# A recurrence's output products in one batch, its scores as 64x64 tiles, and two low-rank gates as split products

## The chip, the cores and the metric

The kernel runs on one core of a Trainium2 chip. The metric is the device time of one execution in microseconds; less is better. The time before is a median of three runs.

## What is computed

One layer of an encoder: sequence 2048, width 1024, float32. The change touches the left one of two parallel head groups, RWKV-7 with 8 heads of 64:

```python
proj = rms_norm(h, norm_mix_w) @ w_in                    # (2048, 1024) @ (1024, 3328)
r, k, v, wd, ad, gd = split(p + (p_prev - p) * mu)       # 512, 512, 512, 64, 64, 128 columns
w_log = -softplus(-(w0 + tanh(wd) @ w_decay_up)) - 0.5   # low-rank gate 1: 64 -> 512
a     = sigmoid(a0 + ad @ a_up)                          # low-rank gate 2: 64 -> 512
g     = sigmoid(gd) @ g_up
S_t   = S_{t-1} (diag(w_t) - kk_t^T (a_t kk_t)) + v_t^T k_t ;   y_t = S_t r_t     # per head
y     = group_norm(y) * lnx_w + lnx_b + bonus ;   out = y * g
```

The other parts (differential attention, attention to memory tokens, an MLP of width 4096 and the norms) are as large or larger and stay as they are.

## The kernel before

The tokens are handled in four blocks of 512. `phase1` (lines 740 to 950) multiplies the normed tokens by `w_in`, one column tile of 128 at a time. Each float32 product there is split in three: weights and tokens are each kept as a high and a low part of type fp32r, and `inproj_stream` (L631, L632, L634) issues high x high, high x low and low x high, each 128x128 by 128x512. This stream of matmuls is the bulk of the stage; a generator hands it out one step at a time, and `run` puts pieces of the recurrence between its steps, at fractions of a stage that the pieces yield.

The recurrence works on units: a block has two units, each of two pairs (p = 0, 1) of heads, and a pair holds two heads on 64 partitions each (`hs`). So there are 8 units and 16 pairs. A unit goes through `prep` (features, scores, transposes, the inverse of a triangular matrix, merge) and, a stage later, `finish` (the scan and the output), while the next unit is in `prep`.

- `rwkv_features` (L286) computes the two gates: `psw` (L291) and `psa` (L300) are one float32 product each per pair, 64 rows deep, with `lwa` holding `w_decay_up` on partitions 0 to 63 and `a_up` on 64 to 127, and `wad` the gates' inputs likewise. The tile `wad` comes from `lead0` at the head of each block. The features `BK` are written for a head in two steps, `BK[hs, :, h]` (L323) and then `BK[hs, :, 1 - h]` (L324).
- `rwkv_scores` (L349) makes, for 4 chunks of 64 tokens at a time and each head, one product `BK` x `AR` of 64 rows, 128 output rows and 128 columns (L359), and masks it on VectorE into `A` (L362). The quarter of `A` that lies in the other head's rows and the first 64 columns is not used from here: `rwkv_merge` (L502) writes columns 0 to 63 of all rows again.
- `rwkv_scan` (L505) runs over the 8 chunks of a unit. For each chunk and pair: `se` is the state times a decay (L521, ScalarE, one instruction a head); `psu` is `A` x `UV` (L524); `psy` gets its first term, `AR` x state (L526); `psu` is copied into `UV` (L528); then `pss` is `BKt` x `UV` (L534), `psy` gets its second term, `A` x `UV` (L536), and the new state is written to `UV` of the next chunk (L542, VectorE, one instruction a head). Chunk c+1 needs the state of chunk c. `psy` is needed by `rwkv_out` alone, after the scan.
- `prep_x` (L231) transposes and norms the next block's tokens (L247, L254); while it runs, the stream of that block has no input.

A float32 product is two MATMUL records in the trace ("passes" below), an fp32r product is one. The order of instructions on each engine is set at build time by a planner that works with priorities (`urgent`, `high_priority`) and its own estimate of times; on the chip every engine then runs its list in order. Tiles with the same `tag` share buffers, and a later tile waits until an earlier one is no longer read.

## Time and profile before

| | |
|---|---|
| time before, median of 3 runs | 3757.99 us (3751.84 to 3759.37) |
| the profiled execution: its own time | 3768.81 us |
| the profiled execution: span from first to last instruction | 3767.1 us |
| TensorE (PE) matmul busy | 3581.6 us, 95% |
| VectorE (DVE) busy | 1957.9 us, 52% |
| ScalarE (ACT) busy | 1720.5 us, 46% |
| GpSimd (POOL) busy | 1464.5 us, 39% |
| mean granted TensorE clock | 0.968 of 2.4 GHz |

Phase 1 with the recurrence takes about the first 1250 us. "Busy" of TensorE is from records whose ends overlap, so the cost of a matmul is read from when the next one starts. In the timeline a row is one or more instructions of the same line in a row: start, duration of the whole group, line, operation, tiles, rows * columns of the array in use, size of the moving operand and count.

### The profile page before, as it was taken

What the parts mean: (1) busy time and instruction counts of PE and PEld (TensorE: products, weight loads), DVE (VectorE), ACT (ScalarE), POOL (GpSimd) and SP (SyncE); (2) the same over time, 40 slices, a digit from 0 to 9 for tenths busy, and PEclk for the clock granted to TensorE, in tenths of its full rate; (3) what the DMA queues carried; (4) which work ended last, traced back from release to release, by engine and by line L of the source; (5) the groups of instructions that cost most, each with busy time, mean ns of one, the idle gap of its engine ahead of it and who ended that gap; (6) DMA issues with size and microseconds to landing.
All of it is one profiled execution on the core that took longest, in us unless ns stands there. A gap on an engine that the chain in (4) does not pass through costs nothing. (4 is left out here: it accounts for less than half of the span.)

```text
span 3767.1 us, 57886 instructions
## 1 busy us (share of the span) xinstructions
PE 3581.6 (95%) x21297; PEld 2871.5 (76%) x21297; DVE 1957.9 (52%) x4093; ACT 1720.5 (46%) x3802; POOL 1464.5 (39%) x1195
## 2 busy tenths in 40 slices
PE   7999999999999878899999989999999999999998
PEld 5767766767777767678787777888878888888887
DVE  4456666666574636465566756666634332313132
ACT  5364464454455626554455765555543421212123
POOL 4424324423434534344435435343353332222225
PEclk9989999999999899999999999999999999999999
DMA  4343342333335674343324425232243331111113
GB/s 149 107 128 88 82 127 84 86 107 88 87 88 160 207 210 142 106 121 93 113 79 118 139 73 144 79 112 78 85 152 94 111 102 48 48 51 48 48 57 108
DMA packets 566066, 390.52 MB, mean 104 GB/s; under 512 B 65187, under 2 KB 491254, under 8 KB 565782
## 3 DMA queue, kind: packets, MB, share of 16 engines
q1 hardware_dynamic: 534134, 329.55, 30.5%
q10 hardware_dynamic: 28064, 50.35, 4.0%
q0 software_dynamic: 3584, 6.92, 0.8%
q8 instruction: 168, 2.75, 0.3%
q14 instruction: 116, 0.95, 0.1%
HBM read 311.14 MB, written 75.56 MB: 103 GB/s over the span
## 5 line engine op out<-in xcount | busy, mean ns | idle before, releaser
L170 POOL TENSOR_TENSOR wlo<-wraw,whi 128x512 fp32r<-128x512 f32 x520 | 689.5, 1327 | 1247.6 <-ACT whi L169 1218.6
L616 POOL TENSOR_TENSOR wlo<-wraw,whi 128x512 fp32r<-128x512 f32 x288 | 413.8, 1438 | 597.4 <-ACT whi L615 479.3
L169 ACT ACTIVATE whi<-wraw 128x512 fp32r<-128x512 f32 x520 | 327.9, 631 | 639.9 <-PE ps_dn L187 327.0
L186 PE MATMUL ps_dn<-hdh,whi 128*128 128x512 f32 x1024 | 402.1, 393 | 2.3 <-DVE t L1408 1.2
L187 PE MATMUL ps_dn<-hdl,whi 128*128 128x512 f32 x1024 | 401.8, 393 | 0.3 <-DVE hdl L1413 0.3
L188 PE MATMUL ps_dn<-hdh,wlo 128*128 128x512 f32 x1024 | 398.8, 393 | 3.3 <-POOL wlo L170 3.1
L186 PE MATMUL ps_up<-h2h,whi 128*128 128x512 f32 x1024 | 400.1, 391 | 1.0 <-DVE t L1408 0.9
L187 PE MATMUL ps_up<-h2l,whi 128*128 128x512 f32 x1024 | 400.7, 391 | 0.0
L188 PE MATMUL ps_up<-h2h,wlo 128*128 128x512 f32 x1024 | 395.3, 391 | 0.8 <-POOL wlo L170 0.8
L631 PE MATMUL ps_acc<-xhi,whi 128*128 128x512 f32 x832 | 343.7, 414 | 20.0 <-ACT carry L278 18.9
L634 PE MATMUL ps_acc<-xhi,wlo 128*128 128x512 f32 x832 | 343.8, 414 | 2.2 <-POOL wlo L616 2.0
L632 PE MATMUL ps_acc<-xlo,whi 128*128 128x512 f32 x832 | 340.3, 409 | 0.0
L615 ACT ACTIVATE whi<-wraw 128x512 fp32r<-128x512 f32 x288 | 181.2, 630 | 273.4 <-PE ps_acc L632 98.0
L1422 DVE TENSOR_TENSOR ht<-ht,ps_dn 128x512 f32<-128x512 f32 x128 | 87.8, 686 | 347.3 <-PE ps_dn L188 347.2
L1048 ACT ACTIVATE pt<-ps_s,nmx 128x512 f32<-128x512 f32 (+3 forms) x320 | 198.4, 621 | 142.4 <-DVE nmx L1047 117.9
L1047 DVE TENSOR_REDUCE nmx<-ps_s 128x1 f32<-128x512 f32 (+3 forms) x320 | 192.5, 606 | 75.6 <-PE ps_s L1044 71.6
L188 PEld LDWEIGHTS ps_dn<-hdh,wlo 128*128 128x128 f32 x1024 | 193.1, 189 | 45.3 <-POOL wlo L170 6.4
L186 PEld LDWEIGHTS ps_dn<-hdh,whi 128*128 128x128 f32 x1024 | 193.0, 188 | 41.8 <-issue 1.6
L186 PEld LDWEIGHTS ps_up<-h2h,whi 128*128 128x128 f32 x1024 | 192.1, 188 | 41.3 <-DVE t L1408 1.6
L187 PEld LDWEIGHTS ps_dn<-hdl,whi 128*128 128x128 f32 x1024 | 193.2, 189 | 39.8 <-DVE hdl L1413 0.5
L188 PEld LDWEIGHTS ps_up<-h2h,wlo 128*128 128x128 f32 x1024 | 192.4, 188 | 40.3 <-POOL wlo L170 1.5
L187 PEld LDWEIGHTS ps_up<-h2l,whi 128*128 128x128 f32 x1024 | 192.3, 188 | 38.8
(336 smaller groups left out, 7772.4 us busy)
## 6 DMA issues: line engine op xcount, KB each, us to landing
wraw<-in_w_in_dram SPq DMA_DIRECT2D x208, 256.0 KB
wraw<-in_w_down_dram SPq DMA_DIRECT2D x208, 256.0 KB
wraw<-in_w_up_dram SPq DMA_DIRECT2D x192, 256.0 KB
s_hT<-xt ACTq DMA_DIRECT2D x64, 256.0 KB
wraw<-in_w_out_dram SPq DMA_DIRECT2D x56, 256.0 KB
s_qkvT<-qkv ACTq DMA_DIRECT2D x48, 256.0 KB
wraw<-in_w_mq_dram SPq DMA_DIRECT2D x48, 256.0 KB
wraw<-s_mb SPq DMA_DIRECT2D x48, 256.0 KB
```

The source lines that it names most:

```text
L169: nc.scalar.activation(out=hi, in_=raw, func=AF.Copy)
L170: nc.gpsimd.tensor_tensor(out=lo, in0=raw, in1=f32(hi), op=ALU.subtract)
L186: nc.tensor.matmul(ps, whi(k), ahi(k), start=(k == 0), stop=False)
L187: nc.tensor.matmul(ps, whi(k), alo(k), start=False, stop=False)
L188: nc.tensor.matmul(ps, wlo(k), ahi(k), start=False, stop=(k == nk - 1))
L615: nc.scalar.activation(out=hi, in_=raw, func=AF.Copy)
L616: nc.gpsimd.tensor_tensor(out=lo, in0=raw, in1=f32(hi), op=ALU.subtract)
L631: nc.tensor.matmul(o, hi[:, kk, :], xs[k][0], start=(k == 0), stop=False)
L632: nc.tensor.matmul(o, hi[:, kk, :], xs[k][1], start=False, stop=False)
L634: nc.tensor.matmul(o, lo[:, kk, :], xs[k][0], start=False, stop=last)
L1047: nc.vector.tensor_reduce(out=nmx[:, m, c:c + 1], in_=ps[:, 0:w], axis=AX.X, op=ALU.max, negate=True)
L1048: nc.scalar.activation(out=pt[:, cw(c)], in_=ps[:, 0:w], func=AF.Exp, bias=nmx[:, m, c:c + 1], accum_out=sm[:, m, c:c + 1])
```

## The change

- **Scan.** The two `psy` products leave the loop over chunks. The state at the start of every chunk is kept in a new tile `Sv` (128 x 8 x 64), written by one more VectorE instruction per chunk and pair, and `se` is read from it with one instruction for both heads. After the last chunk, all 16 `AR` x `Sv` products of a pair and then all 16 `A` x `UV` products are issued into `psy`. The scan yields two more steps, and the start of `rwkv_out` in `finish` moves from 17 to 19 units of `fscan`.
- **Scores.** The product of 128 output rows becomes two of 64: rows of the same head with all 128 columns, and rows of the other head with the last 64 columns alone. The mask becomes two instructions as well.
- **Gates.** `lead0` splits the gates' inputs into `wads`, two tiles with the high part on one half of the partitions and the low part on the other. `lora_load` keeps each second-layer weight twice over on 128 rows, as a high and a low tile. A gate product is then two fp32r matmuls 128 rows deep.
- The descriptor memory of GpSimd's DMAs is set to 2048 bytes.

```diff
+def lora_mm(g, ps, i, cs, wad):
+    for j in range(2):
+        g.nc.tensor.matmul(ps, g.lora[i][j][:, cs], wad[i], start=(j == 0), stop=(j == 1))
 def rwkv_features(...):
-    nc.tensor.matmul(psw, g.lwa[0:64, cs], wad[0:64, :], start=True, stop=True)
+    lora_mm(g, psw, 0, cs, wad)
-    nc.tensor.matmul(psa, g.lwa[64:128, cs], wad[64:128, :], start=True, stop=True)
+    lora_mm(g, psa, 1, cs, wad)
 def rwkv_scores(...):
-                nc.tensor.matmul(pss[h][:, cc, :], u.BK[hs, c, :, :]..., u.AR[hs, c, :, :]..., start=True, stop=True)
+                vs = slice(64 - 64 * h, 128 - 64 * h)
+                nc.tensor.matmul(pss[h][hs, cc, :], u.BK[hs, c, h, :], u.AR[hs, c, :, :]..., start=True, stop=True)
+                nc.tensor.matmul(pss[h][vs, cc, 64:128], u.BK[hs, c, 1 - h, :], u.AR[hs, c, 1, :], start=True, stop=True)
-            nc.vector.tensor_tensor(out=u.A[:, 4 * c4:4 * c4 + 4, h, :], in0=pss[h], in1=g.mask..., op=ALU.mult)
+            nc.vector.tensor_tensor(out=u.A[hs, cs, h, :], in0=pss[h][hs], in1=g.mask[hs...], op=ALU.mult)
+            nc.vector.tensor_tensor(out=u.A[vs, cs, h, 64:128], in0=pss[h][vs, :, 64:128], in1=g.mask[vs...], op=ALU.mult)
 def rwkv_scan(...):
+        u.Sv = sp.tile([P, NCK, CH], F32, tag=f"Sv{p}", name="Sv", bufs=1)
+        nc.scalar.activation(out=u.Sv[:, 0, :], in_=g.S[hp], func=AF.Copy)
-            for hs in H:
-                nc.scalar.activation(out=u.se[hs, :], in_=u.UV[hs, c, hs], func=AF.Copy, scale=u.EC[hs, c:c + 1])
+            nc.scalar.activation(out=u.se, in_=u.Sv[:, c, :], func=AF.Copy, scale=u.EC[:, c:c + 1])
-                nc.tensor.matmul(u.psy[hs, c, :], u.AR[hs, c, 1, :], u.UV[hs, c, hs], start=True, stop=False)
-                nc.tensor.matmul(u.psy[hs, c, :], u.A[:, c, h, 64:128], u.UV[:, c, hs], start=False, stop=True)
+                nc.vector.scalar_tensor_tensor(out=u.Sv[:, c + 1, :], in0=pss, scalar=u.EC[:, c:c + 1], in1=u.se, ...)
+    for p in range(2):
+        u.psy = g.ps_y.tile([P, NCK, CH], F32, tag=f"y{p}", name=f"psy{p}")
+        for c in range(NCK):
+            for hs in H:
+                nc.tensor.matmul(u.psy[hs, c, :], u.AR[hs, c, 1, :], u.Sv[hs, c, :], start=(c == 0), stop=False, ...)
+        for c in range(NCK):
+            for h, hs in enumerate(H):
+                nc.tensor.matmul(u.psy[hs, c, :], u.A[:, c, h, 64:128], u.UV[:, c, hs], start=False, stop=True, ...)
+        yield
 def lead0(blk):
-                t = pool.tile([P, TB], F32, tag="wad", name="wad", bufs=1)
+                t = pool.tile([P, TB], F32, tag="mix", name="wad", bufs=2)
+                for i, (r, o) in enumerate(((slice(0, 64), slice(64, 128)), (slice(64, 128), slice(0, 64)))):
+                    w = pool.tile([P, TB], F32R, tag=("wad", "wad1")[i], name="wads", bufs=1)
+                    nc.scalar.activation(out=w[r, :], in_=t[r, :], func=AF.Copy)
+                    nc.vector.tensor_tensor(out=w[o, :], in0=t[r, :], in1=f32(w[r, :]), op=ALU.subtract)
 def lora_load():
-            g.lwa = g.cst.tile([P, TB], F32, name="lwa")
-            nc.sync.dma_start(out=g.lwa[0:64, :], in_=g.i.w_decay_up[0])
-            nc.sync.dma_start(out=g.lwa[64:128, :], in_=g.i.a_up[0])
+            for nm, src in (("w", g.i.w_decay_up), ("a", g.i.a_up)):
+                raw = pool.tile([P, TB], F32, tag="mix", name="lraw", bufs=2)
+                for r in (0, 64):
+                    nc.sync.dma_start(out=raw[r:r + 64, :], in_=src[0])
+                nc.scalar.activation(out=hi, in_=raw, func=AF.Copy)
+                nc.gpsimd.tensor_tensor(out=lo, in0=raw, in1=f32(hi), op=ALU.subtract)
 def finish(u, sc=1.0):
-            t = 0.01 + g.fscan * 17
+            t = 0.01 + g.fscan * 19
-    nc = _bacc.Bacc("TRN2", target_bir_lowering=False, num_devices=1)
+    nc = _bacc.Bacc("TRN2", target_bir_lowering=False, num_devices=1, dynamic_dma_scratch_size=2048)
```

## Rows read from the trace of the kernel before

**Rows 1.** Busy time by stretch: PE, PEld, DVE, ACT, POOL, granted clock, DMA share, GB/s.
```profile
0.00:1200.00 1200.00, 1131.91 (x9333) 838.50 (x9333) 712.87 (x1794) 588.78 (x1411) 457.17 (x426) 0.95 0.37 105
```
**Rows 2.** Waits of PE, 100 to 1200 us: total, times, longest.
```profile
PE ps_acc L631 <- ACT carry L278: 13.8, 9, 2.1
```
**Rows 3.** Timeline of PE around two turns of the scan (start, duration, line, tiles, count).
```profile
391.95 0.39 PE L631 MATMUL ps_acc<-xhi,whi 128*128 128x512 f32 x1
392.18 0.40 PE L632 MATMUL ps_acc<-xlo,whi 128*128 128x512 f32 x1
392.50 0.34 PE L524 MATMUL psu<-UV,A 128*64 128x64 f32 x4
392.77 0.33 PE L526 MATMUL psy<-UV,AR 64*64 64x64 f32 x4
393.03 0.50 PE L634 MATMUL ps_acc<-xhi,wlo 128*128 128x512 f32 x1
...
393.69 0.32 PE L526 MATMUL psy<-UV,AR 64*64 64x64 f32 x2
393.95 0.34 PE L524 MATMUL psu<-UV,A 128*64 128x64 f32 x4
```
**Rows 4.** PE by line, 0 to 1300 us: count of passes, busy us, mean ns, idle before.
```profile
L359 PE MATMUL ps_sc<-AR,BK 64*128 64x128 f32 x512 | 74.0, 309 | 4.3 <-DVE A L362 3.9 <-ACT ta L302 0.4
L526 PE MATMUL psy<-UV,AR 64*64 64x64 f32 x512 | 67.0, 248 | 0.2
L536 PE MATMUL psy<-UV,A 128*64 128x64 f32 x512 | 54.4, 239 | 3.2 <-ACT UV L528 3.2
```
**Rows 5.** Timeline of PE, a turn of the scan with pss and the second psy term.
```profile
508.79 0.34 PE L534 MATMUL pss<-UV,BKt 128*64 128x64 f32 x4
508.95 0.29 PE L536 MATMUL psy<-UV,A 128*64 128x64 f32 x4
509.17 0.50 PE L634 MATMUL ps_acc<-xhi,wlo 128*128 128x512 f32 x1
```
**Rows 6.** DVE and ACT by line, 0 to 1300 us (columns of rows 4).
```profile
L362 DVE TENSOR_TENSOR A<-ps_sc,mask 128x512 f32<-128x512 f32 x64 | 43.0, 689 | 64.7 <-PE ps_sc L359 64.2
L538 DVE SCALAR_TENSOR_TENSOR S<-pss,EC,se 128x64 f32<-128x64 f32 x16 | 4.4, 277 | 8.5 <-PE pss L534 4.3 <-PE psy L536 4.1
...
L521 ACT ACTIVATE se<-UV,EC 64x64 f32<-64x64 f32 x256 | 88.5, 346 | 45.4 <-DVE UV L542 40.6 <-ACT se L521 0.2
```
**Rows 7.** Timeline of PE, one gate product and the next stream matmul.
```profile
354.13 1.12 PE L291 MATMUL psw<-wad,lwa 64*128 64x512 f32 x2
355.18 0.50 PE L632 MATMUL ps_acc<-xlo,whi 128*128 128x512 f32 x1
```
**Rows 8.** Timeline of PE, the stream's first wait after the start.
```profile
43.36 0.77 PE L631 MATMUL ps_acc<-xhi,whi 128*128 128x512 f32 x1 [5.13 <-ACT carry L278]
```
**Rows 9.** Timeline of PE, scores of both heads in one run, then of one.
```profile
400.18 1.16 PE L359 MATMUL ps_sc<-AR,BK 64*128 64x128 f32 x16
401.27 0.51 PE L634 MATMUL ps_acc<-xhi,wlo 128*128 128x512 f32 x1
...
511.50 1.16 PE L359 MATMUL ps_sc<-AR,BK 64*128 64x128 f32 x8
512.59 0.34 PE L524 MATMUL psu<-UV,A 128*64 128x64 f32 x4
```
**Rows 10.** Timeline of PE, 64x64 products on all four quarters of the array.
```profile
199.29 1.16 PE L500 MATMUL psw<-T,BK 64*64 64x64 f32 x64
```
**Rows 11.** Busy time by stretch, sum of the four stretches without stream (columns of rows 1).
```profile
sum 135.30, PE 121.64 PEld 87.15 DVE 107.02 ACT 93.81 POOL 19.98; mean PE 30.41 PEld 21.79 DVE 26.75 ACT 23.45 POOL 4.99
```
**Rows 12.** Timeline of PE, the stream after 3.7 us of small products.
```profile
385.40 0.63 PE L631 MATMUL ps_acc<-xhi,whi 128*128 128x512 f32 x1
385.82 0.63 PE L632 MATMUL ps_acc<-xlo,whi 128*128 128x512 f32 x1
```
**Rows 13.** DMAs that GpSimd issues: count, size, median us to landing.
```profile
LD<-A POOLq DMA_DIRECT2D x16, 128.0 KB, 2.9
```

More of the change, by code (lines that the diff above doesn't have):

```diff
@@ L358, in rwkv_scores @@
                 hs = slice(64 * h, 64 * h + 64)
-                nc.tensor.matmul(pss[h][:, cc, :], u.BK[hs, c, :, :].rearrange("p a t -> p (a t)"),
+                vs = slice(64 - 64 * h, 128 - 64 * h)
+                nc.tensor.matmul(pss[h][hs, cc, :], u.BK[hs, c, h, :],
                                  u.AR[hs, c, :, :].rearrange("p a t -> p (a t)"), start=True, stop=True)
+                nc.tensor.matmul(pss[h][vs, cc, 64:128], u.BK[hs, c, 1 - h, :], u.AR[hs, c, 1, :], start=True, stop=True)
+        cs = slice(4 * c4, 4 * c4 + 4)
         for h in range(2):
-            nc.vector.tensor_tensor(out=u.A[:, 4 * c4:4 * c4 + 4, h, :], in0=pss[h],
-                                    in1=g.mask[:, None, :].to_broadcast([P, 4, P]), op=ALU.mult)
+            hs, vs = slice(64 * h, 64 * h + 64), slice(64 - 64 * h, 128 - 64 * h)
+            nc.vector.tensor_tensor(out=u.A[hs, cs, h, :], in0=pss[h][hs],
+                                    in1=g.mask[hs, None, :].to_broadcast([64, 4, P]), op=ALU.mult)
+            nc.vector.tensor_tensor(out=u.A[vs, cs, h, 64:128], in0=pss[h][vs, :, 64:128],
+                                    in1=g.mask[vs, None, 64:128].to_broadcast([64, 4, 64]), op=ALU.mult)
         yield
@@ L510, in rwkv_scan @@
         u, hp = us[p], pairs[p]
+        u.Sv = sp.tile([P, NCK, CH], F32, tag=f"Sv{p}", name="Sv", bufs=1)
         for hs in H:
             nc.scalar.activation(out=u.UV[hs, 0, hs], in_=g.S[hp][hs, :], func=AF.Copy)
+        nc.scalar.activation(out=u.Sv[:, 0, :], in_=g.S[hp], func=AF.Copy)
     yield
-    for p in range(2):
-        us[p].psy = g.ps_y.tile([P, NCK, CH], F32, tag=f"y{p}", name=f"psy{p}")
     for c in range(NCK):
@@ L524, in rwkv_scan @@
                 nc.tensor.matmul(psu[hs, :], u.A[:, c, h, 0:64], u.UV[:, c, hs], start=True, stop=True)
-            for h, hs in enumerate(H):
-                nc.tensor.matmul(u.psy[hs, c, :], u.AR[hs, c, 1, :], u.UV[hs, c, hs], start=True, stop=False)
             for h, hs in enumerate(H):
@@ L534, in rwkv_scan @@
                 nc.tensor.matmul(pss[hs, :], u.BKt[:, c, hs], u.UV[:, c, hs], start=True, stop=True)
-            for h, hs in enumerate(H):
-                nc.tensor.matmul(u.psy[hs, c, :], u.A[:, c, h, 64:128], u.UV[:, c, hs], start=False, stop=True)
             if c == NCK - 1:
@@ L543, in rwkv_scan @@
                                                    in1=u.se[hs, :], op0=ALU.mult, op1=ALU.add)
+                nc.vector.scalar_tensor_tensor(out=u.Sv[:, c + 1, :], in0=pss, scalar=u.EC[:, c:c + 1],
+                                               in1=u.se, op0=ALU.mult, op1=ALU.add)
+        yield
+    for p in range(2):
+        u = us[p]
+        u.psy = g.ps_y.tile([P, NCK, CH], F32, tag=f"y{p}", name=f"psy{p}")
+        for c in range(NCK):
+            for hs in H:
+                nc.tensor.matmul(u.psy[hs, c, :], u.AR[hs, c, 1, :], u.Sv[hs, c, :], start=(c == 0), stop=False,
+                                 skip_group_check=True)
+        for c in range(NCK):
+            for h, hs in enumerate(H):
+                nc.tensor.matmul(u.psy[hs, c, :], u.A[:, c, h, 64:128], u.UV[:, c, hs], start=False, stop=True,
+                                 skip_group_check=True)
         yield
@@ L783, in post @@
             def post(ps):
-                t = pool.tile([P, TB], F32, tag="wad", name="wad", bufs=1)
+                t = pool.tile([P, TB], F32, tag="mix", name="wad", bufs=2)
                 mix_tile(g, pool, 12, ps, t, blk)
                 nc.scalar.activation(out=t[0:64, :], in_=t[0:64, :], func=AF.Tanh)
-                st[blk][1] = t
+                pair = []
+                for i, (r, o) in enumerate(((slice(0, 64), slice(64, 128)), (slice(64, 128), slice(0, 64)))):
+                    w = pool.tile([P, TB], F32R, tag=("wad", "wad1")[i], name="wads", bufs=1)
+                    nc.scalar.activation(out=w[r, :], in_=t[r, :], func=AF.Copy)
+                    nc.vector.tensor_tensor(out=w[o, :], in0=t[r, :], in1=f32(w[r, :]), op=ALU.subtract)
+                    pair.append(w)
+                st[blk][1] = pair
             return Item(blk, w_in(12), post, pre)
```

4 lines of the change are left out of this document (added).

## The prediction

> **What bounds the kernel now.** I read the stages first, then the waits of TensorE, then its timeline. In the first 1200 us, where the recurrence runs, TensorE is busy for 1131.9 us, VectorE for 712.9, ScalarE for 588.8 and GpSimd for 457.2 [rows 1]. The longest kind of wait of TensorE between 100 and 1200 us is 13.8 us in all [rows 2]. So a microsecond taken off TensorE's list there should come off the end, and the other engines have room, on average. Busy time hides what a small product costs, since records overlap; I take the time from one start to the next. The stream's matmuls start 0.23 us apart (391.95, 392.18) [rows 3]. A turn of the scan that stands between them costs more than its four passes: from the stream matmul at 392.18 to the one at 393.03 there are 0.85 us, where 0.23 would do, and the next one is some 0.1 us longer than usual [rows 3]. Every change of the array's shape has a price: a pass of these lasts about 0.24 us by itself [rows 4], so in a group of four that lasts 0.34 the last one started 0.10 us after the first, and the next shape began 0.15 us or more after that (392.50 to 392.77) [rows 3]. In a long run the step is smaller: 64 passes on four quarters of the array last 1.16 us [rows 10], (1.16 - 0.24) / 15 = 0.06 us for each on a quarter.
>
> **The y products leave the loop.** The first term has 512 passes [rows 4], four to a turn, so 128 turns. Where the four stand together they cost 0.26 us (392.77 to 393.03); where the two heads fall on either side of `psu` each half costs 0.26 us (393.69 to 393.95) [rows 3]. Walking the order of matmuls I count 203 groups of L526, so 203 x 0.26 = 53 us go. The second term, also 512 passes [rows 4], has the shape of `pss`, next to which it stands: a pair of passes costs 0.06 us, four 0.12 (from 508.95 to 509.17 are 0.22 us with the step back to the stream, which `pss` alone would pay too) [rows 5]; 128 x 0.12 = 15, and 16 with some groups that stand apart. The number of visits to the scan does not fall: `psu` and `pss` stay. What is added is a batch for each of the 16 pairs: 16 couples of passes at 0.06 for each term is 1.9 us, two shape changes 0.3 and the second-pass delays 0.1, so 2.3 us, 37 in all (34 if both pairs of a unit share a visit, 45 if the stream cuts in). Net: -53 - 16 + 37 = -32 us. The batch stands before `rwkv_out` of the unit alone, whose start the change moves later; nothing on TensorE waits for that but the tail of the last unit, so I add nothing.
>
> The first-term couples write one PSUM bank from two row halves. The trace has that already: four passes on both halves take 0.33 us as a group, two on one half 0.32 [rows 3], so they run side by side. The Trainium skill, TensorEngine Tiling (Array Packing), section Restrictions and Gotchas, says that row tiles cannot access one bank at the same time; by that rule each couple would take twice 0.06 us. The trace does not agree with it here.
>
> **VectorE and ScalarE in the scan.** 112 writes of `Sv` are added, at 0.28 us as the 128x64 update (L538), 31 us; 128 of the 256 `se` instructions go, at 0.35 us, 44 us off ScalarE; 16 copies come [rows 6]. VectorE's next instruction behind an `Sv` write is the other pair's state, and its `psu` waits 0.28 us more; the stream covers that while there is one.
>
> **The gates.** One product takes 1.05 us now (354.13 to 355.18) [rows 7]; each of 16 pairs has one for either gate: 32 x 1.05 = 33.6 us. Two stream-like matmuls at 0.23 [rows 3] are 0.46, in all 14.7, and they need no change of shape beside the stream: -19, of which 1 goes back since scan turns that now share a visit with a gate get one of their own: -18 us (-23 to -14). The splits in `lead0` are two instructions on ScalarE and two on VectorE for each of four blocks, ahead of products that come a stage later; the stream covers them. At the start, two more DMAs stand on SP's queue ahead of the first weights, and the first two normed tiles of `prep_x`, which share the tag `mix`, wait until GpSimd has made the low parts. Behind that comes a wait of 5.13 us of TensorE for ScalarE [rows 8], which can take up the delay: 0 to +5, I take +2.
>
> **Scores.** A head's eight passes of 128 columns cost 1.09 us as a run, and sixteen passes of both heads cost the same 1.09 (511.50 to 512.59, 400.18 to 401.27) [rows 9]: what counts is the length of one quarter's list. The new list of a quarter is eight passes of 128 columns, so it gets no shorter; the second product has its own quarter and can run beside it, as all four quarters do in L500 [rows 10]. The shape is cheaper to enter and leave by some 0.1 us a run; 69 runs are -7 us. But the second product needs the features of L324, the first those of L323 alone. If it is issued after the first it costs its eight passes at 0.06 and possibly a visit of 0.4 us, 0.87 together, for 64 heads of 4 chunks: up to +56. Near the gate of the features I expect a fifth of them to stand alone, +11 - 7, so +4. The 64 masks become 128 instructions; the added ones are bounded by the 128x64 and the 128x512 rows, 0.28 and 0.69 us [rows 6], I take 0.45: 29 us on VectorE.
>
> **Where there is no cover.** Four stretches of 26 to 40 us, where `prep_x` runs and the stream has no input, hold 28% of the scan's passes. There VectorE is busy for 107 of 135 us, TensorE for 122 [rows 11]. Of the 69 us taken off, 19 lie there; VectorE gets 28% of 31 + 29, so 17 us, and would stand at 124 of 135. I let half of TensorE's gain be lost there: +9 (0 to +28).
>
> **The clock.** After 3.7 us of small products the stream's matmuls are 0.43 us apart instead of 0.23 [rows 12]: the granted clock is at 1.2 GHz, half of 2.4, for some 3.4 us, and 1.6 us are lost. The batch of a unit is 4.5 us of small products. If each of eight brought that on: +13; the scan's shorter turns could save as much as 5. I take +4.
>
> **GpSimd's DMAs.** The smaller descriptor memory shows in no row. If each of its DMAs had to wait for the one before, that is some 2.9 us a piece [rows 13] in the chain of the inverse, which the stream covers; none to +10, I take 0, as TensorE waits little for that chain.
>
> **The sum.** -32 (y) - 18 (gates) + 2 (start) + 4 (scores) + 9 (no cover) + 4 (clock) = -31 us against the profiled execution's 3768.8. That one is 0.3% over the median of 3758, so the prediction is 3758 - 31 = **3727 us**.
>
> **Rivals.** (1) *Everything converts*: the heads' scores run side by side, the clock holds, the uncovered stretches shrink with TensorE. Then -32 - 18 - 7 = -57, 3701 us. For it: TensorE's 122 of 135 us; against it VectorE's load there. (2) *The uncovered stretches turn into VectorE's*: they lose all of the 19 us and grow by the 17 that VectorE gets, with the clock's +13: -32 - 18 + 2 + 4 + 36 + 13 = +5, 3763 us, no change. (3) *Slower: the second score product stands by itself.* The place is L359's successor in `rwkv_scores`, the price 0.87 us for each of 64. It takes up the gain without scores, 35 us, from 40 of 64 on, and the kernel is measurably slower from 49 of 64; with all, 3758 - 35 + 56 = 3779 us. For it: L324 is an instruction of 512 elements like the mask, some 0.69 us [rows 6], long enough for the first product's run to begin before it ends; against it: for the second group of four chunks all features are there. (4) *The batch does not run in couples*, two row halves taking turns at one bank: 16 pairs x 16 couples x 0.06 = +15 us, 3742 us; the groups of four and of two speak against it [rows 3]. This is the case that the Trainium skill's sentence above would make.
>
> **Chances.** The forecast with its own range of 3712 to 3748, in which (4) lies too, 0.58, of which (4) has 0.04; (1) 0.12; (2) 0.17; (3) 0.13. A difference under 0.2%, 7.5 us, can't be told from no change by this measurement. So faster 0.70, within 0.17, slower 0.13. The range that leaves 2 in 10 out runs from (1)'s end to just past (2): 3698 to 3767.
>
> **What would show it.** Right: scan visits of `psu` alone at four passes; the y products in 16 runs of some 2.3 us; gate products as two matmuls 0.23 apart; VectorE's idle time gone in the four stretches, which keep their length within 5 us. Wrong: score passes of the second kind in runs of their own; half clock right behind each batch; a stage after phase 1 that is longer than before, which would mean that the planner's new order, not the products, decides.

## The result, and the profile after

The changed kernel takes 3785.0 us (3780.2 to 3787.7, four runs) against 3758.7 us (3751.8 to 3764.8) of the kernel before beside it: a ratio of 1.0062, 95% interval 1.0033 to 1.0090, so some 23 us slower. The forecast was 3727 us with a range to 3767. The profiled execution has a span of 3782.5 us and a mean granted clock of 0.957 (before 3767.1 and 0.968). The profiled execution of the kernel before took 3768.81 us, 10 us more than its median, so between the two profiles there are only 15 us.

The first 1200 us by engine, columns as in [rows 1]:

```profile
0.00:1200.00 1200.00, 1089.64 (x9537) 822.06 (x9539) 760.33 (x1944) 538.37 (x1282) 448.25 (x420) 0.91 0.36 102
```

TensorE is busy for 42 us less than in [rows 1] and ScalarE for 50 less; VectorE has 47 us more. The granted clock has fallen from 0.95 to 0.91. So TensorE's list did get shorter, and the time went into gaps and into periods at a lower clock.

PE by line, 0 to 1300 us (columns of [rows 4]):

```profile
L365 PE MATMUL ps_sc<-AR,BK 64*64 64x128 f32 x512 | 78.0, 327 | 6.1 <-ACT ss L345 2.5 <-ACT ta L307 2.0 <-DVE BK L328 0.9
L367 PE MATMUL ps_sc<-AR,BK 64*64 64x64 f32 x512 | 56.5, 269 | 0.0
L534 PE MATMUL psu<-UV,A 128*64 128x64 f32 x512 | 47.1, 266 | 17.4 <-DVE Sv L550 17.3
L558 PE MATMUL psy<-Sv,AR 64*64 64x64 f32 x512 | 47.0, 264 | 0.4 <-DVE y L576 0.4
L562 PE MATMUL psy<-UV,A 128*64 128x64 f32 x512 | 25.4, 232 | 0.0
```

`psu` now waits 17.3 us, in 18 waits that end with VectorE's write of `Sv`; in the kernel before it had no such wait. The writes and the masks in two parts, by line of VectorE, 0 to 1300 us:

```profile
L371 DVE TENSOR_TENSOR A<-ps_sc,mask 64x512 f32<-64x512 f32 x64 | 43.8, 685 | 38.5 <-PE ps_sc L367 38.1
L550 DVE SCALAR_TENSOR_TENSOR Sv<-pss,EC,se 128x64 f32<-128x64 f32 x112 | 31.8, 284 | 1.6
L373 DVE TENSOR_TENSOR A<-ps_sc,mask 64x256 f32<-64x256 f32 x64 | 27.0, 422 | 1.4
```

Two turns of the scan in the timeline of PE (columns of [rows 3]):

```profile
515.13 0.34 PE L534 MATMUL psu<-UV,A 128*64 128x64 f32 x4
515.40 0.33 PE L558 MATMUL psy<-Sv,AR 64*64 64x64 f32 x4
515.66 0.34 PE L534 MATMUL psu<-UV,A 128*64 128x64 f32 x4
515.92 0.33 PE L558 MATMUL psy<-Sv,AR 64*64 64x64 f32 x4
```

The first y term stands behind `psu` just as in [rows 3]. In the text of the kernel it comes after the loop, but its operands are ready in the loop, and the planner has put many of them back: of the 152 runs of L558 (L526 had 203) 92 are groups of four passes, and 79 of these stand right behind `psu`. Of the second term most is a batch, here with 28 of a pair's 32 passes:

```profile
272.35 0.33 PE L558 MATMUL psy<-Sv,AR 64*64 64x64 f32 x4
272.61 1.04 PE L562 MATMUL psy<-UV,A 128*64 128x64 f32 x28
```

The gates came as predicted: matmuls 0.23 us apart behind the first, in place of 1.05 us for each product [rows 7]:

```profile
362.64 0.50 PE L288 MATMUL psw<-wads,lwh 128*128 128x512 f32 x1
362.97 0.39 PE L288 MATMUL psw<-wads,lwl 128*128 128x512 f32 x1
363.20 0.39 PE L288 MATMUL psw<-wads,lwh 128*128 128x512 f32 x1
```

The four stretches without stream, columns of [rows 1]. First the rows of the kernel before, of which [rows 11] has the sum, then those of the changed kernel:

```profile
222.50:256.70 34.20, 31.44 (x213) 23.63 (x211) 29.23 (x53) 21.85 (x56) 3.81 (x3) 0.63 0.49 157
510.00:545.60 35.60, 32.59 (x275) 23.15 (x273) 29.89 (x57) 24.32 (x65) 5.40 (x7) 0.85 0.47 145
800.90:826.70 25.80, 21.97 (x231) 15.35 (x229) 17.58 (x37) 19.42 (x48) 4.43 (x6) 0.97 0.67 180
1071.00:1110.70 39.70, 35.65 (x330) 25.02 (x329) 30.31 (x81) 28.22 (x84) 6.34 (x9) 0.80 0.38 95
```

```profile
225.40:264.00 38.60, 31.22 (x252) 21.87 (x250) 36.91 (x81) 23.01 (x62) 2.65 (x3) 0.62 0.49 151
514.40:551.60 37.20, 27.41 (x229) 19.47 (x227) 34.47 (x73) 19.92 (x53) 2.74 (x3) 0.63 0.52 156
806.70:834.70 28.00, 21.66 (x184) 15.46 (x182) 27.54 (x60) 17.73 (x46) 1.62 (x1) 0.64 0.41 136
1081.50:1127.80 46.30, 37.91 (x338) 25.85 (x336) 42.51 (x107) 26.50 (x80) 5.11 (x7) 0.59 0.24 67
sum 150.10, PE 118.19 PEld 82.65 DVE 141.43 ACT 87.16 POOL 12.13; mean PE 29.55 PEld 20.66 DVE 35.36 ACT 21.79 POOL 3.03
```

They are 15 us longer, VectorE (third figure) is busy for 141 of 150 us, and the clock, which had fallen far only in the first of them, is at 0.59 to 0.64 in all four: TensorE runs at 1.2 GHz there for most of the time. TensorE is idle for 32 of the 150 us (14 of 135 before); by its waits, some 18 us of that are for VectorE and some 10 for ScalarE, the longest 4.6 us. Waits are not all there is to it: in the first stretch of the kernel before the clock was at 0.63 as well, with this one wait (total, times, longest):

```profile
PE ps_xt L247 <- DVE xn L254: 2.8, 1, 2.8
```

In the whole profile the time at 1.2 GHz rose from 241 to 325 us, and single periods of 17 us or more, of which there was one, are now four, one in each stretch. The later phases keep their length: from the last 128x512 product of the first stream to the end there are 2352 us before and 2348 after.

### The profile page after: what moved, and what is told of

It reads as the page before. It is cut to its first block, busy times and chain, and to the rows that moved or that the text cites. A ratio compares the mean times of both kernels' runs of the same rounds, so it can differ in the third digit from the quotient of the medians.

```text
span 3782.5 us, 58913 instructions
## 1 busy us (share of the span) xinstructions
PE 3562.5 (94%) x21809; PEld 2872.0 (76%) x21809; DVE 2011.5 (53%) x4277; ACT 1676.9 (44%) x3700; POOL 1465.9 (39%) x1197
```

## The experiments

Every kernel was compared with the kernel before on the same chip (whose median differs between chips, 3757 to 3768 us). In the table, **lost** is (1 - mean granted clock) x span, median over the executions, as a difference to the kernel before (for the changed kernel, to the profiled execution of before): what the time at 1.2 GHz takes from TensorE's cycles, whether it needed them or not. **Rest** is the difference of the medians less that. The last three columns come from the one profiled execution, up to the start of the last 128x512 product of the first stream: idle time of PE, half of the time at 1.2 GHz, and what is left, TensorE's work at full clock. Idle time that lies at 1.2 GHz is in both of the last two columns: 13 us in the kernel before, 33 in the changed one, so work comes out up to some 10 us too low where that is much. For kernels whose TensorE products are the same the work differs by some 10 us (before, e_deadsv, e_shift, e_nofwd: 1232 to 1243) to 20 (e_ybatch, e_svpool, e_seuv: 1203 to 1223), so differences under 10 us say nothing, and those under 20 little.

| kernel | ratio, 95% interval | lost | rest | work | idle | half |
|---|---|---|---|---|---|---|
| before | 1 | 0 | 0 | 1234 | 100 | 82 |
| changed | 1.0062 (1.0033 to 1.0090) | +38 | -12 | 1172 | 140 | 123 |
| e_ybatch | 1.0077 (1.0057 to 1.0097) | +27 | 0 | 1214 | 127 | 96 |
| e_yforce | 1.0085 (1.0064 to 1.0107) | +37 | -4 | 1208 | 128 | 106 |
| e_lora | 0.9993 (0.9979 to 1.0008) | +19 | -21 | 1216 | 102 | 97 |
| e_scores | 1.0002 (0.9985 to 1.0020) | -4 | +3 | 1237 | 109 | 61 |
| e_noar | 1.0026 (1.0013 to 1.0040) | +34 | -24 | 1174 | 135 | 108 |
| e_ar2 | 1.0068 (1.0048 to 1.0089) | -16 | +47 | 1262 | 117 | 70 |
| e_nosv | 1.0017 (1.0004 to 1.0031) | +11 | -3 | 1211 | 123 | 87 |
| e_svpool | 1.0007 (0.9995 to 1.0020) | +2 | +1 | 1223 | 110 | 77 |
| e_seuv | 1.0057 (1.0036 to 1.0079) | +37 | -11 | 1203 | 117 | 116 |
| e_deadsv | 1.0019 (1.0006 to 1.0032) | -2 | +9 | 1232 | 113 | 79 |
| e_shift | 0.9965 (0.9949 to 0.9981) | -8 | -2 | 1240 | 98 | 72 |
| a_noy | 1.0032 (1.0017 to 1.0047) | +27 | -13 | 1216 | 103 | 114 |
| a_noy17 | 1.0054 (1.0038 to 1.0071) | +35 | -12 | 1213 | 114 | 111 |
| a_svpool | 1.0031 (1.0017 to 1.0045) | +31 | -16 | 1188 | 133 | 113 |
| a_log | 1.0065 (1.0047 to 1.0083) | +39 | -13 | 1176 | 144 | 120 |
| a_fill | 1.0051 (1.0035 to 1.0067) | +25 | -5 | 1191 | 140 | 116 |
| e_nofwd | 1.0053 (1.0034 to 1.0073) | +29 | -8 | 1243 | 83 | 108 |
| a_nofwd | 0.9963 (0.9949 to 0.9977) | +30 | -43 | 1182 | 104 | 106 |

**The parts alone.** First the scan:

```diff
 rwkv_scan (and finish, descriptor memory) as in the change, scores and gates as before:
-                nc.tensor.matmul(u.psy[hs, c, :], u.AR[hs, c, 1, :], u.UV[hs, c, hs], start=True, stop=False)
-                nc.tensor.matmul(u.psy[hs, c, :], u.A[:, c, h, 64:128], u.UV[:, c, hs], start=False, stop=True)
+                nc.vector.scalar_tensor_tensor(out=u.Sv[:, c + 1, :], in0=pss, ...)
+    for p in range(2):  # behind the loop
+        u.psy = g.ps_y.tile([P, NCK, CH], F32, tag=f"y{p}", name=f"psy{p}")
...
```

> Only the change of the scan (states kept in Sv, both y terms issued behind the loop, unit's output two turns later) with the smaller descriptor memory; scores and gates as before. The prediction's own terms for it: -32 for the products, some +4 of clock and a part of the +9 in the uncovered stretches, so 3730 us (3715 to 3745). Theory A (the trace of the changed kernel shows 92 groups of four passes of psy<-Sv,AR still standing behind psu inside the turns: the scheduler has put the products back into the loop): the products bring next to nothing (154.5 us of PE's starts before, 150.4 after, for psu, pss and both y terms), and what is added on VectorE costs what PE waits for Sv, 17 us: 3760 to 3780. Theory B (the clock: half-clock time of 240.7 us before, 324.6 after, belongs to the batch): also 3780, with the half-clock time up by 60 us or more here. If it is the scores or the gates that lose the time, this run is at 3730 to 3750.

Measured 1.0077, 27 us slower. The scan's change alone loses as much as the whole, and the prediction's 3730 did not come. The accounting gives 20 us less work, 27 more idle time and 14 more lost at half clock. Neither theory fits as it was put: A has the products bring next to nothing, and B wants 60 us or more of added time at 1.2 GHz, where the profile has 29 (241 to 270 us). So the batch was forced:

```diff
+            if c == NCK - 1:
+                us[p].psy = g.ps_y.tile([P, NCK, CH], F32, tag=f"y{p}", name=f"psy{p}")
+                pss = us[p].psy[:, 0, :]
```

> As e_ybatch, but the last turn's pss of each pair is written into the bank of psy, so that no y product can start before the last state is done: the batch is a batch in the order of the instructions too. Prediction's price of a true batch: 3758 - 32 = 3726, with the losses of the uncovered stretches up to 3745. Theory A says 15 to 40 us less than e_ybatch, since 203 groups of the first term leave the turns. If Sv on VectorE in the chain of turns, or the clock, is what costs (theory B), it is no faster than e_ybatch, 3760 to 3785, and PE's waits for Sv stay at 17 us or more.

Measured 1.0085. In PE's timeline the products are a batch now, most of them in runs of 10 to 32 passes:

```profile
433.42 0.91 PE L550 MATMUL psy<-Sv,AR 64*64 64x64 f32 x22
434.26 0.34 PE L535 MATMUL psy<-UV,BKt 128*64 128x64 f32 x4
...
437.08 0.56 PE L550 MATMUL psy<-Sv,AR 64*64 64x64 f32 x12
437.57 1.15 PE L554 MATMUL psy<-UV,A 128*64 128x64 f32 x32
```

The work is 26 us under that of the kernel before, near the 32 predicted, and nothing of it reaches the end. Theory A falls as an explanation of the loss: that the planner puts the products back is true, but undoing it gains nothing. The wait of `psu` for `Sv`, which was to stay at 17 us or more, is 10.6 us here.

The gates alone:

```diff
 lora_mm, lead0, lora_load and descriptor memory as in the change, scan and scores as before:
-    nc.tensor.matmul(psw, g.lwa[0:64, cs], wad[0:64, :], start=True, stop=True)
+    lora_mm(g, psw, 0, cs, wad)
...
```

> Only the gates' change (split weights and split wad, four 128x512 products in place of two fp32 ones for each pair) with the smaller descriptor memory; scan and scores as before. Prediction: -18 and +2 at the start, so 3742 us (3735 to 3751). From the trace of the changed kernel: gate and product starts 11 to 14 us less, the first stream matmul 4.4 us later: 3748. If the scheduler's new order alone is worth more than these, it may lie anywhere in 3740 to 3775, and then the stretch in which it loses is not beside a gate.

Measured 0.9993, no difference, and not the predicted 3742. The work is 18 us less, as predicted, and the rest of the time 21 less; but 19 us are lost to the clock. The four stretches in this kernel:

```profile
222.10:254.30 32.20, 28.39 (x188) 21.65 (x186) 28.62 (x53) 18.99 (x48) 2.32 (x2) 0.63 0.46 139
504.10:537.00 32.90, 29.06 (x189) 21.84 (x187) 29.90 (x56) 21.19 (x52) 2.77 (x3) 0.64 0.51 152
783.30:816.50 33.20, 29.36 (x188) 22.12 (x186) 30.27 (x56) 20.86 (x52) 2.88 (x3) 0.64 0.46 143
1064.80:1111.50 46.70, 44.22 (x262) 29.85 (x260) 33.23 (x78) 26.57 (x80) 6.77 (x9) 0.56 0.29 79
```

The clock is low in all four, as it was in the first alone in the kernel before, though no gate product stands in them and the y products are in the turns as before.

The scores alone:

```diff
 rwkv_scores as in the change, scan, gates and descriptor memory as before:
+                nc.tensor.matmul(pss[h][vs, cc, 64:128], u.BK[hs, c, 1 - h, :], u.AR[hs, c, 1, :], start=True, stop=True)
...
```

> Only the scores' change (a 64x64 product of 128 columns and one of 64 on the other quarter, masks in two parts); scan, gates and descriptor memory as before. Prediction: +4 on PE and 29 us more on VectorE, a quarter of it in the uncovered stretches, so 3765 us (3751 to 3780). Rival 3 (the second product stands by itself): 3758 + 56 = 3814. From the trace of the changed kernel, where the passes of both kinds are mixed within a run but PE's starts are 13.9 us further apart in all: 3772.

Measured 1.0002, no difference. Rival 3 falls: the work is 3 us more, where that rival had 56; the predicted 4 is too small for the accounting to tell from nothing. Here the clock holds in three of the four stretches:

```profile
226.40:268.50 42.10, 37.05 (x292) 27.08 (x290) 32.17 (x60) 25.77 (x70) 3.83 (x3) 0.56 0.46 149
521.70:550.20 28.50, 24.43 (x271) 16.25 (x269) 25.80 (x52) 19.57 (x52) 5.10 (x7) 0.97 0.64 192
802.10:822.70 20.60, 20.23 (x255) 13.48 (x254) 19.58 (x41) 16.84 (x42) 5.04 (x7) 1.00 0.61 184
1070.10:1109.60 39.50, 33.76 (x445) 23.81 (x443) 36.26 (x97) 30.51 (x89) 7.33 (x10) 0.91 0.32 89
```

The rests of the three parts, 0 - 21 + 3 = -18, and their losses to the clock, 27 + 19 - 4 = +42, add up to about what the whole shows (-12 and +38). Their work does not: -20 - 18 + 3 = -35, where the whole has -62.

**What a product in a turn is worth.** The first y term left out, and doubled:

```diff
 e_noar:
-                nc.tensor.matmul(u.psy[hs, c, :], u.AR[hs, c, 1, :], u.UV[hs, c, hs], start=True, stop=False)
 e_ar2:
+                nc.tensor.matmul(u.psy[hs, c, :], u.AR[hs, c, 1, :], u.UV[hs, c, hs], start=True, stop=True)
```

> The kernel before with the first y term (512 passes of psy<-UV,AR) left out and nothing in its place: no Sv, no batch, no shift; y lacks that term. This prices the removal by itself. The prediction has 203 groups x 0.26 = 53 us on PE's list, 19 x 53/69 of them, 15, in the stretches without stream with half lost: -45, so a ratio of 0.988. Theory E (in the turns the products filled time in which PE would wait for ScalarE's UV or VectorE's update anyway, and where they go the wait or the half clock takes their place): at most the part under the stream, 10 to 25 us, ratio 0.993 to 0.998.

> The kernel before with the first y term issued twice (the second issue overwrites the first, so nothing else changes): the mirror of e_noar, 512 passes more in the turns, +53 us by the prediction's price and +59 by e_noar's accounting. If TensorE's list bounds the phase in the covered stretches, +38 to +59: ratio 1.010 to 1.016. Theory E (in the turns such products fill time that is lost anyway): under +20 us, ratio 0.998 to 1.005.

Leaving 512 passes out makes the kernel slower, 1.0026; doubling them makes it slower too, 1.0068. The first 1200 us, e_noar and then e_ar2:

```profile
0.00:1200.00 1200.00, 1100.69 (x8795) 822.49 (x8799) 696.75 (x1779) 578.05 (x1386) 450.58 (x425) 0.92 0.36 104
```

```profile
0.00:1200.00 1200.00, 1115.76 (x9420) 822.84 (x9421) 717.37 (x1774) 569.64 (x1365) 444.53 (x416) 0.96 0.35 101
```

The price of the removal was about right: 59 us of work went, against 53 predicted. But e_noar has 35 us more idle time and 26 more of half clock. Its stream runs ahead, by 34 us at 926 us of the span, and then stops between 936 and 955 us, where PE's timeline has turns of the scan with few other products beside them, and behind them the stream at half clock:

```profile
942.47 0.48 PE L524 MATMUL psu<-UV,A 128*64 128x64 f32 x4 [2.52 <-DVE UV L540]
...
955.90 0.63 PE L632 MATMUL ps_acc<-xhi,wlo 128*128 128x512 f32 x1
956.33 0.63 PE L629 MATMUL ps_acc<-xhi,whi 128*128 128x512 f32 x1
```

By 1003 us the whole lead is gone. For e_noar this is theory E, and stronger than it was put: work taken off brings nothing. e_ar2 lies above E's range (1.005) and below that of TensorE's list (1.010). Its 512 added passes stand in the same 203 groups as the old ones, so no change of shape is added, and they make 28 us of work, not 53; these cost 30 us in time (3795.0 against 3764.5 us).

Part of the idle time has a plain source. `psu` of the next turn needs VectorE's update of `UV`. In the nine kernels that keep both y products in the turns (the kernel before, e_lora, e_scores, e_shift, e_deadsv, e_ar2, a_noy, a_noy17, e_nofwd) `psu` waits for VectorE for 1.7 us at most. Where one or both are left out or issued behind the loop, it waits for some 9 to 19 us in every kernel but e_svpool (2.3), whether VectorE writes `Sv` or not. Three rows show it, of e_noar, which has no `Sv`, of e_yforce, and of e_nosv, which is e_yforce without the writes (45 to 1300 us: total, times, longest):

```profile
PE psu L524 <- DVE UV L540: 9.9, 9, 3.3
PE psu L523 <- DVE Sv L543: 10.6, 13, 2.9
PE psu L523 <- DVE UV L541: 11.2, 12, 4.4
```

So the y products cover a wait, which opens when they go.

**The write of `Sv`.** Four kernels ask what it costs:

```diff
 e_nosv (on e_yforce):
-                nc.vector.scalar_tensor_tensor(out=u.Sv[:, c + 1, :], in0=pss, ...)
 e_svpool (on e_ybatch): that line out, and for each head
+                nc.gpsimd.tensor_copy(out=u.Sv[hs, c, :], in_=u.UV[hs, c, hs])
 e_seuv (on e_ybatch): se from UV by two instructions, Sv still written by VectorE
 e_deadsv (on the kernel before):
+                nc.vector.scalar_tensor_tensor(out=u.Sv[:, c + 1, :], in0=pss, ...)
```

> As e_yforce (3790 us), with the writes of Sv inside the turns left out: the first term reads the unit's first state for every chunk, and se is made from it too, so this part of the output isn't the reference's. TensorE has the same work as in e_yforce. Theory D: the loss goes, and what TensorE saved in the covered stretches shows: 3758 - 26 + 10 = some 3740 (3725 to 3755). Theory B: TensorE still has less to do in the turns, the clock stays low, 3775 to 3795.

> As e_ybatch, but Sv is copied from UV by GpSimd (two 64x64 copies a turn and pair) instead of a third update on VectorE; se is made from UV by two instructions, as before. GpSimd is busy for 11 of 131 us in the four stretches. ScalarE's overwriting of UV now waits for the copies. Theory D: the time falls from 3784 to some 3745 to 3760, unless GpSimd's copies are longer than psu and then stand in the chain of the turn themselves, 256 of them, 128 turns: with 0.2 us more for each uncovered turn (28% of 64 in a row) 4 to 10 us more. Theory B: 3775 to 3795.

> As e_ybatch (ratio 1.0077), but se is made from UV by two instructions of ScalarE, as before, while VectorE still writes Sv as a third update. It differs from e_svpool (ratio 1.0007) only in who writes Sv. If the third update on VectorE is the cause by itself (theory D), as e_ybatch: 1.005 to 1.009. If it is that ScalarE, in order, waits with se for Sv ahead of the copies of UV, as e_svpool: 0.999 to 1.003.

> The kernel before with its products where they were, plus the 112 writes of Sv on VectorE, which nothing reads, and the smaller descriptor memory. 112 x 0.28 = 31 us of VectorE in all, and psu's bank comes free one write later. Theory D (VectorE: in e_ybatch it is busy for 122.9 of the 131.3 us of the four stretches without stream, where it was 107.0 of 135.3): the time rises by 15 to 30 us although no TensorE work has gone, 3772 to 3788. Theory B (the clock falls since TensorE has less to do): here TensorE has all its work, so no change, 3750 to 3765.

Without the write e_yforce's 1.0085 becomes 1.0017 (e_nosv); with the write on GpSimd e_ybatch's 1.0077 becomes 1.0007 (e_svpool); with it on VectorE again, and `se` made as before, 1.0057 (e_seuv). In three comparisons of kernels whose y products have left the turns, the third update on VectorE goes with 0.5 to 0.7%, 19 to 26 us. e_nosv also makes `se` from an early state, so the first comparison takes a second wait out of the turn; the last, e_seuv against e_svpool, differs in the text only in who writes `Sv`. e_svpool and e_seuv lie where theory D had them, e_nosv between what D and B expected. GpSimd has room for it, by its row of e_svpool:

```profile
L521 POOL COPY Sv<-UV 64x64 f32<-64x64 f32 x256 | 73.7, 289 | 161.7 <-DVE UV L538 119.7 <-ACT UV L513 33.5
```

In all three the difference lies in the loss to the clock (37 to 11, 27 to 2, 37 to 2 us). In the kernel before the same dead write costs only 7 us (e_deadsv), with the clock unmoved, where theory D had 15 to 30. So the write is not dear by itself, and its price depends on the kernel it stands in. That it makes TensorE's products sparse, and the clock falls for that, would fit but isn't shown: in e_lora the clock falls with all y products in the turns and no write. And without the write, the scan's change still gains nothing (1.0017, 1.0007).

**Controls: what a new order alone does.**

```diff
 e_shift (on the kernel before): two empty yields at the end of rwkv_scan, and
-            t = 0.01 + g.fscan * 17
+            t = 0.01 + g.fscan * 19
 a_noy (on the changed kernel): rwkv_scan as before with the two yields; a_noy17: without them, fscan * 17
```

> The kernel before with nothing changed but what the scan's change carries along: two empty steps at the end of the scan, the unit's output two steps later in the planner's dues, and the smaller descriptor memory. If the later output or the descriptor memory is the cause (theory C), some +20 to +27 us as in e_ybatch, so 3775 to 3785. If the added write on VectorE is the cause (theory D) or the missing TensorE work and its clock (theory B), no change: 3750 to 3765.

> The changed kernel with the scan as before (both y terms inside the turns, no Sv), the unit's output two steps later and the smaller descriptor memory: gates, scores and the shift. By the single runs (0.9993, 1.0002, 0.9965) their sum is 0.996, 15 us under the kernel before. If the parts don't add, since each new order of the scheduler has its own luck, 0.996 to 1.003.

> The changed kernel with the scan and the unit's output step as before: gates and scores alone together. If the parts add: 0.9993 x 1.0002, so 0.9995 (0.997 to 1.002). If gates and scores together are what a_noy showed (1.0032) and the shift does nothing for them: 1.003, and then it is not one part but the order the scheduler makes for this pair, with the split first product a stage later at the start (4.5 us).

e_shift, which has the instructions of the kernel before in another order (and the smaller descriptor memory), is faster than both kernels: 0.9965, interval 0.9949 to 0.9981. Gates and scores, which are nothing alone (0.9993, 1.0002), cost 0.5% together (1.0054, above what either expectation allowed), with 35 us lost to the clock and 12 gained in the rest; with the shift 0.3%. So the parts don't add in time, and an order that is changed by an edit elsewhere can move the clock in the stretches by as much as the edit is worth. It also means that the changed kernel (1.0062) is about as slow without its new scan (1.0054): the loss can't be laid on the scan, or on the write of `Sv`, alone. Theory C falls.

**On the changed kernel.**

```diff
 a_svpool: Sv by GpSimd and se from UV, as in e_svpool
 a_log (prep_x):
-        eng = nc.gpsimd if blk == 0 and k % 2 else nc.vector
+        eng = nc.gpsimd if k % 2 else nc.vector
 a_fill (prep_x, ahead of the transposes):
+        for _ in range(3 if blk and k else 0):
+            nc.tensor.matmul(ps, out[-1][0][:, 0:P], out[-1][0], start=True, stop=True)
```

> The changed kernel with Sv copied from UV by GpSimd and se made from UV, everything else of the change kept. Theory D: 26 us less than the changed kernel, ratio to the kernel before 0.998 to 1.001. If the loss of the whole has another source beside it (masks on VectorE), it stays above 1.003.

> The changed kernel with half of prep_x's low parts (odd k) on GpSimd in all blocks, not in the first alone: 12 instructions of 0.69 us, 8 us, leave VectorE's list in three of the stretches without stream, where VectorE is busy for 141 of 150 us and GpSimd for 12. TensorE's list is untouched. Theory D/F (VectorE's list sets the length of these stretches): 5 to 15 us less than the changed kernel (ratio 1.006), so 1.002 to 1.005, and these stretches shorter by that. If the clock or the order sets it: 1.005 to 1.008.

> The changed kernel with 21 idle products of 128x512 added to each of three prep_x (three ahead of each group of transposes, overwritten by these), 63 x 0.23 = 14 us of TensorE work at full clock, 27 at half. Theory B (what is lost is lost through the clock: TensorE has too little to do in these stretches): the granted clock rises there from 0.6 and the time falls, ratio under 1.004. Theory F (VectorE's list sets these stretches): the clock may rise, the time stays: 1.005 to 1.009. If TensorE bounds them: 14 to 27 us more, 1.010 to 1.013.

a_svpool gains half of what e_svpool did (1.0031), and its interval overlaps with that of the changed kernel; its loss to the clock stays at 31 us, where e_svpool had 2. a_log shortens the four stretches as expected, by their sum:

```profile
sum 134.90, PE 99.58 PEld 68.33 DVE 123.13 ACT 86.83 POOL 24.36; mean PE 24.89 PEld 17.08 DVE 30.78 ACT 21.71 POOL 6.09
```

15 us less than 150.1, but the kernel is no faster (1.0065). This agrees with VectorE's list setting the length of these stretches, but their length does not set the time: new gaps of the stream come elsewhere (956 to 971, 1139 to 1152 us). a_fill raises the clock in three of them:

```profile
226.90:280.70 53.80, 44.16 (x455) 30.47 (x453) 46.66 (x103) 29.68 (x82) 5.23 (x7) 0.81 0.38 111
524.10:572.20 48.10, 43.77 (x500) 31.14 (x498) 40.42 (x106) 26.42 (x69) 6.80 (x8) 0.82 0.40 113
811.70:853.20 41.50, 38.85 (x466) 28.34 (x465) 38.81 (x100) 24.50 (x65) 6.80 (x8) 0.88 0.44 122
1079.80:1132.80 53.00, 41.79 (x406) 28.49 (x405) 45.56 (x128) 25.98 (x78) 6.77 (x9) 0.65 0.27 70
```

and 14 us or more of added products cost nothing: 13 us less are lost to the clock than in the changed kernel, and the time stays (1.0051), as theory F had it and not theory B (under 1.004). The stretches are not the same ones, though: they last 196 us in all, 46 more than in the changed kernel, and hold 1827 matmuls in place of 1003, of which the filler is 63. A higher clock in them did not bring time here.

**A shorter chain.** Last, the forward substitution on VectorE was left out on both sides:

```diff
 rwkv_inverse, in e_nofwd on the kernel before and in a_nofwd on the changed one:
-    for i, _ in enumerate(ginter(steps(24, 32, tmp), 62, steps(0, 24, tmp2), 46)):
-        if i % 6 == 5:
-            yield
+    for i in range(18):
+        yield
```

> The kernel before with the 31+23 steps of the forward substitution on VectorE left out in each of 8 units (108 instructions, 31 us of VectorE, 38 to 40 us from first to last), so T isn't the reference's; TensorE's list, DMAs and all else stay. Theory H (the chain that prepares a unit sets the period of 139 us): the period falls by up to 38 us, until TensorE's own 1234 us bound it: 60 to 130 us less, ratio 0.965 to 0.984. If TensorE's list with its idle and half-clock time bounds the stage: no change, ratio 0.995 to 1.005. If VectorE's list in the stretches without stream does: the substitution mostly lies outside them, 0 to 15 us less.

> The changed kernel with the same steps left out. Theory H: with the chain short, the 62 us that the change takes off TensorE show: this run is 20 to 60 us faster than e_nofwd. If the change's cost is VectorE's added work (Sv, masks) in its chain of turns, it stays behind e_nofwd by 15 us or more as it does now (24). If the order made by the scheduler decides, anything between.

e_nofwd is slower than the kernel before, 1.0053, although 198 us of VectorE's 713 in the first 1200 are gone. Theory H, with its 60 to 130 us less, falls for the kernel before. The first 1200 us, e_nofwd and then a_nofwd:

```profile
0.00:1200.00 1200.00, 1151.49 (x9249) 857.49 (x9249) 514.62 (x923) 584.23 (x1397) 414.90 (x418) 0.92 0.36 102
```

```profile
0.00:1200.00 1200.00, 1121.05 (x9933) 851.93 (x9933) 568.70 (x1127) 564.27 (x1342) 430.63 (x433) 0.92 0.38 108
```

Its idle time is the least of all, its clock has fallen (29 us lost, four long periods at 1.2 GHz where the kernel before has one). And on this base the change gains what was forecast, 31 us: from 1.0053 to 0.9963 it is 33 us faster, as theory H expected of this pair, with the clock at 0.92 in both. Where the clock is down on both sides, and VectorE has room, the 61 us less of work bring 33.

## Why the prediction was wrong

**Right.** *The gates:* -18 predicted, 18 us less work in e_lora, matmuls 0.23 us apart. *The scores:* +4 predicted, +3 measured, both under what the accounting resolves; the second products are mixed into the runs of the first, and rival 3 did not come. *The price of the first term:* -53 predicted, -59 of work in e_noar. *GpSimd's DMAs:* 0 predicted; e_lora, e_shift and e_deadsv have the smaller descriptor memory and lie at 0.9965 to 1.0019. *The end of phase 1 decides:* the later phases are as long as before, and the planner's order did not lengthen a stage behind it.

**Rival 4** did not come. In the batch of e_yforce 22 passes on two row halves last 0.84 us to the next start and 12 last 0.49: (0.84 - 0.49) / 10 = 0.035 us a pass, 0.07 a couple, where 0.06 was predicted for couples side by side and twice that for taking turns. The Trainium skill, TensorEngine Tiling (Array Packing), section Restrictions and Gotchas, says that row tiles can't use one bank at the same time; these rows do not agree with it.

**The start.** +2 predicted; the first stream product starts at 29.0 us in place of 24.65, behind a wait of 3.25 us for the normed tile, 4.4 us late, and the stream is still 4.0 us late at its hundredth product.

**The premise.** "So a microsecond taken off TensorE's list there should come off the end": this step failed by itself. e_noar takes 59 us off that list, adds nothing, and is 10 us slower where 45 less were expected. That is a difference of 55, more than a new order of instructions has moved any kernel here. The prediction read the step from TensorE's busy time and its longest kind of wait, 13.8 us [rows 2]; but short waits in the kernel before do not show which waits the products cover.

**The y products leave the loop.** -32 predicted, and the step failed twice. They leave the loop only in the kernel's text: the planner, which the prediction treats as the one who decides about stages, also decides about single products, and put the first term back (92 groups of four). And where they do leave it, 26 us less work brought a kernel 0.85% slower. That the change doesn't do what it says was not among the rivals; it should have been, since a planner that orders by readiness can undo a move in the text.

**VectorE and ScalarE in the scan.** The prediction lets the write of `Sv` cost nothing beyond 17 us of VectorE in the stretches, "the stream covers that while there is one". With the y products out of the turns the runs put 19 to 26 us on this write, in the kernel before 7; and the wait of `psu` that opens there (9.9 us in e_noar) comes without the write as well.

**Where there is no cover.** +9 predicted (0 to +28): a loss of half of TensorE's gain there. VectorE's load in the four stretches rose by 34 us, not 17, to 141 of 150 us, idle time of PE by 41 us in the phase. Rival 2 had the right kind, VectorE's bound, but ended at 3763; and in a_log its rule, stretch length sets the time, doesn't hold either.

**The clock.** This is the term that was most mis-sized: +4 predicted (-5 to +13), +38 by the mean clock, of which the phase has 41 by the table and 31 while TensorE is busy. The prediction looked for half clock behind the batches [rows 12]; it came in the stretches without stream, where the kernel before held 0.85, 0.97 and 0.80 in three of four. [rows 11] gives only the sum of the four rows; a reader of the rows themselves would have seen that the kernel before had something to lose there. The Trainium skill, TensorE: Matmul & The Clock Gate, section HAM oscillation — how this bites in real kernels, describes a kernel whose short bursts of matmuls, each behind a long wait for a DMA, start at the half clock time after time. The trace agrees only in that the half clock comes back in each stretch, at 0.59 to 0.64: the waits are for VectorE and ScalarE here, they make 32 of 150 us, and the first stretch of the kernel before is at 0.63 with 2.8 us of waiting.

With the measured terms the sum is -62 of work, +41 idle, +41 at half clock: +20 at the end of the phase's stream (with idle time at 1.2 GHz counted once, -52, +41 and +31). The profiled executions as a whole are 15 us apart, the medians 26.

**What stays open.** The loss to the clock goes with the time in most kernels (not in e_lora, e_ar2 and a_nofwd), and in e_nofwd and a_nofwd, where it is equal, the change's gain shows. That a lower clock is the cause, not a companion of the waits, isn't shown: a_fill brought 13 us of clock back and spent some 14 on the filler. Nor is it settled why the clock falls with the gates alone or without the forward substitution, where VectorE has no more to do, and why gates and scores together cost what neither does. What is shown is that the premise failed and where the time went; what brings the clock down, and with it which of the edits is to blame for the 23 us, stays open. Every kernel here has its own order of instructions, none holds the order fixed; a difference of under some 20 us between two of them, the 19 us of the write among them, can be the order's.

## What to carry to other kernels

In a kernel that mixes a stream with a dependent chain, TensorE at 95% busy does not mean that work taken off it comes off the end: leave the term out altogether and time that before building its replacement. Read the granted clock stretch by stretch, and ask of each stretch at full clock what keeps it there; small products that fill waits may be worth more than they cost. Where a planner orders instructions by readiness, look at the order it makes, and expect any edit to move the time by a few tenths of a per cent on its own.

## What the runs showed of the hardware that was not expected

The clock often falls for most of a stretch: periods at 1.2 GHz of 17 us or more number one or two in the kernel before, e_scores, e_shift, e_ar2, e_deadsv and e_svpool (ratios 0.9965 to 1.0068), and three to six in e_nosv, e_lora, e_ybatch, e_yforce, e_noar, e_seuv, e_nofwd, a_nofwd and all kernels built on the change but a_fill, which has two. A copy of 64x64 on GpSimd takes 0.289 us (e_svpool), as long as VectorE's update of that size in the kernel before:

```profile
L542 DVE SCALAR_TENSOR_TENSOR UV<-pss,EC,se 64x64 f32<-64x64 f32 x224 | 63.3, 282 | 167.6 <-PE pss L534 157.0 <-PE psy L536 3.3 <-ACT qkv L822 1.0
```

So a small side copy can be handed to GpSimd: e_svpool, which does that, is at 1.0007, where e_ybatch was at 1.0077. And what a product costs TensorE hangs on its neighbours: leaving the 203 groups of the first y term out takes 59 us of work away, doubling the passes within the same groups adds 28.
